# Second-layer weight sums paced at one per tick beside the memory heads, and no VectorE marks for sums among the value products

## The chip, the cores and the metric

The kernel runs on one core of a Trainium2 chip. The metric is the device time of one execution in microseconds. A core has TensorE (PE; weight loads are listed as PEld), VectorE (DVE), ScalarE (ACT), GpSimd (POOL) and SyncE (SP), each working through its own instructions in order, and 16 DMA engines that carry the transfers which SP and POOL issue. SP's transfers lie on a hardware queue (q1 in the profile), POOL's on a software queue (q0).

## The reference

Two post-norm layers over a sequence of 512 rows of width 2048. Each layer multiplies the stream by one wide input matrix and splits the result over three groups of heads; all outputs are gated, joined, projected and normalised:

```python
h = jnp.einsum('bsd,dn->bsn', x, w_in)
(fq, fk, fv, fg, f_logit, dq, dk, dv, dg, iq, ik, iw, mq, mg) = jnp.split(h, offsets, axis=-1)
# 6 forgetting heads: causal softmax with a cumulative log-forget bias
# 6 sparse heads: rotary q and k; an indexer of 16 heads chooses the keys of each query
# 4 memory heads: cross attention into mem (256 rows), whose k and v come from mem @ w_mem_kv
y = jnp.concatenate([y_fox * silu(fg), y_dsa * silu(dg), y_mem * silu(mg)], axis=-1)
y = jnp.einsum('bsn,nd->bsd', y, w_out)
return layer_norm(ALPHA * x + y, ln_gain, ln_bias)
```

## The kernel before

**Precision and chunks.** Every weight comes from DRAM as a chunk of 128 x 2048 fp32 (1 MB). `load_w` (L241) fetches it on SP's queue into a tile `raw` (three buffers). `split_w` makes of each half a rounded part `whi` (ACT, L213) and a remainder `wlo` (DVE, L214), four buffers each; `product` (L220 to L222) multiplies with three matmuls, hi x hi, hi x lo and lo x hi. Loads run two chunks ahead of the products, splits three halves.

**Stages of a layer.** Memory keys and values, small columns, the indexer's queries (stage "index"), the queries and gates of the four memory heads ("mem"), the values and other columns as large products ("values", kind `vs`), the remaining heads ("heads"), the output projection ("out"). The tuple `now` holds the layer and the stage.

**The value products.** These 512-column blocks are computed with seven products of sums of blocks where eight of plain blocks would be needed. That takes sums of weight blocks as right-hand sides. Some are formed in DRAM ahead of time: `weight_sums` copies a block into a DRAM tile `sum` (L376) and adds a second block by a DMA that accumulates (L358, 1 MB). Per layer the values need 32 such transfers: T3, eight copies and eight additions, then T1, likewise. T3 serves the product P7, T1 serves Q5, which comes after the first ten chunks of all four pairs. The two other right-hand sides are grown in place: when P7's chunk has been split, `grow_w` adds the next block into the same `raw` tile by an accumulating DMA (L249), which makes Q6's operand, and once more for Q4. A pair's first ten chunks are P1, P1, P7, P7, P2, Q6, Q6, P2, Q4, Q4; a value chunk holds 24 matmuls.

**What orders the DMAs of POOL.** POOL issues its DMAs in program order: weight sums, grows, the stores of value blocks (L874) and, in layer 1, the stores of the residual rows (L969). So that a sum is not issued long ahead of the place in the program where it stands, `pool_waits` puts a tiny copy on DVE (L348, the mark) and a tiny POOL operation that reads it (L349, seen) ahead of each sum. POOL then goes on only when DVE has come to that place.

**Pace.** `all_sums` is a generator that is stepped by `tick`. The main loop ticks twice per chunk; the sums skip the tick in a chunk's middle in the stages "out" and "values". After each sum `paced` yields the number of ticks until the next: two in "index" of layer 1 and one in "index" of layer 0, three in "out", one in "heads", two in "values", and in "mem" the expression that the change edits: `1 + now[0] * n % 2` is 1 in layer 0, and in layer 1 alternately 2 and 1.

**Layer 1 alone.** During "index" and "mem" of layer 1 `residual_rows` takes layer 0's normalised output through SBUF: SP loads 256 KB (L977), DVE multiplies and adds (L967, L968), POOL stores it (L969), 16 tiles, one every two ticks, with eight rows of gains and biases (L922).

Of the kernel before, what the change touches and what calls it, by code (L numbers as in the profile page):

```python
# [172 lines left out]
def kernel(  # L173
# [25 lines left out]
    def uid(name):  # L199
        count[0] += 1  # L200
        return f"{name}_{count[0]}"
# [7 lines left out]
    def small(name, w, bufs=3):  # L209
        return tiny.tile([P, w], F32, tag=name, name=uid(name), bufs=bufs)  # L210
# [134 lines left out]
    def pool_waits():  # L345

        mark, seen = small("mark", 1), small("seen", 1)
        nc.vector.tensor_copy(mark, mhalf)  # L348
        nc.gpsimd.tensor_tensor(seen, mark, mhalf, op=ALU.mult)  # L349
# [4 lines left out]
    def block(kind, l, pair, g, step):  # L354
        return wall[where[kind, l, 2 * pair + step[1], 2 * step[0] + g]]

    def add_weights(key, src):
        nc.gpsimd.dma_start(sums[key], src, accum_op=ALU.add, max_dma_last_dim=4 * DM)  # L358

    def weight_sums(kind, l, names, pairs):  # L360

        for name in names:
            for n, step in enumerate(SUM_STEPS[name]):
                for pair in pairs:
                    for g in range(2):
                        key = (kind, l, name, pair, g)
                        if isinstance(step, str):
                            src = sums[kind, l, step, pair, g]
                        else:
                            src = block(kind, l, pair, g, step)  # L370
                        pool_waits()
                        if n:
                            add_weights(key, src)
                        else:
                            sums[key] = dram.tile([P, DM], F32, name=uid("sum"))
                            nc.gpsimd.dma_start(sums[key], src)  # L376
                        yield

    def paced(gen, steps=2):

        n = 0
        for _ in gen:
            n += 1
            while now[1] == "kv":
                yield 1
            yield {"mem": 1 + now[0] * n % 2, "heads": 1, "out": 3, "index": 1 + now[0]}.get(now[1], steps)

    def all_sums():


        for l in range(DEPTH):
            yield from paced(weight_sums("val", l, ("T3", "T1"), range(PAIRS)))
            while now != (l, "heads"):
                yield 1
            yield from paced(weight_sums("out", l, ("T3", "T1", "T2", "T4"), range(2)))
# [7 lines left out]
    now = (0, "index")  # L403
# [646 lines left out]
    for i, (kind, l, j, col, _) in enumerate(chunks):  # L1050
# [28 lines left out]
        for h in range(2):  # L1079
            n = 2 * i + h  # L1080
# [135 lines left out]
        if kind == "mv" and l > 0:  # L1216
            now = (l, "kv")
        if kind == "small":
            now = (l, "index")
# [3 lines left out]
        if kind == "mq" and j == 0:  # L1223
            now = (l, "mem")
        if kind == "vs":
            now = (l, "values")
# [17 lines left out]
        if kind == "out" and step == col == 0:  # L1244
            now = (l, "out")
        if kind == "fq" and j == EARLY:
            now = (l, "heads")
# [111 lines left out]
```

## Time and profile before

| | |
|---|---|
| median of 3 runs | 1935.96 us (1935.47 to 1936.17) |
| the profiled execution's own time | 1936.96 us |
| its span, first to last instruction | 1934.6 us |
| mean granted clock of TensorE | 0.994 |
| busy: PE, PEld, DVE, ACT, POOL | 1907.3, 1624.6, 1389.3, 969.2, 356.0 us |
| marks (L348) and their reads on POOL (L349) | 128 each |
| weight sums: copies (L376) and additions (L358) | 64 each |

A row of the timeline gives the start and the length in us, engine, line, operation, what is written and read, and in brackets how long the engine stood idle ahead of it and whom it waited for. Grouped rows give a count (x), the busy time and the mean of one. In the table by stretches each engine's busy time stands with its number of instructions; then the granted clock of TensorE, the mean busy share of the 16 DMA engines, and GB/s. Line numbers are those of the kernel before; the change adds one line at L371, so in its own rows the lines behind have numbers one higher.

### The profile page before, as it was taken

What the parts mean: (1) busy time and instruction counts of PE and PEld (TensorE: products, weight loads), DVE (VectorE), ACT (ScalarE), POOL (GpSimd) and SP (SyncE); (2) the same over time, 40 slices, a digit from 0 to 9 for tenths busy, and PEclk for the clock granted to TensorE, in tenths of its full rate; (3) what the DMA queues carried; (4) which work ended last, traced back from release to release, by engine and by line L of the source; (5) the groups of instructions that cost most, each with busy time, mean ns of one, the idle gap of its engine ahead of it and who ended that gap; (6) DMA issues with size and microseconds to landing.
All of it is one profiled execution on the core that took longest, in us unless ns stands there. A gap on an engine that the chain in (4) does not pass through costs nothing.

```text
span 1934.6 us, 25323 instructions
## 1 busy us (share of the span) xinstructions
PE 1907.3 (99%) x9282; PEld 1624.6 (84%) x9282; DVE 1389.3 (72%) x2343; ACT 969.2 (50%) x1538; POOL 356.0 (18%) x615
## 2 busy tenths in 40 slices
PE   9999999999999999999999999899999999999997
PEld 8998888888888888888899988678888888888886
DVE  6666656779665667788867877367786656677898
ACT  6564454445444555645475644344454445555553
POOL 0231201111132111110142202111111331112101
PEclk9999999999999999999999999999999999999999
DMA  9699888787988778988778967898889887789856
GB/s 369 227 293 330 203 200 230 237 236 244 265 266 229 237 241 232 271 322 300 241 268 251 300 222 214 190 255 243 230 247 262 257 236 240 238 238 260 348 195 154
DMA packets 110712, 484.57 MB, mean 250 GB/s; under 512 B 11504, under 2 KB 44272, under 8 KB 69500
## 3 DMA queue, kind: packets, MB, share of 16 engines
q0 software_dynamic: 32864, 216.05, 44.7%
q1 hardware_dynamic: 77724, 266.90, 38.0%
q8 instruction: 73, 1.20, 0.2%
q14 instruction: 51, 0.42, 0.1%
HBM read 445.14 MB, written 174.09 MB: 320 GB/s over the span
## 4 chain that ended last, share of the span: by engine, by line
PE 90%; DVE 4%; DMA 2%; ACT 2%; issue 1%; POOL 0%; SPq 0%; DVEq 0%; ACTq 0%; POOLq 0%
PE c L220 12%; PE c L222 12%; PE c L221 12%; PE v L220 11%; PE v L222 11%; PE v L221 11%; PE z L221 4%; PE z L222 4%; PE z L220 4%; DMA raw<-in_wall_dram 2%; PE pt L681 1%; DVE wlo L214 1%; PE ix L599 1%; PE ix L598 1%; PE po L222 1%
## 5 line engine op out<-in xcount | busy, mean ns | idle before, releaser
L214 DVE TENSOR_TENSOR wlo<-raw,whi 128x1024 fp32r<-128x1024 f32 (+1 forms) x497 | 607.1, 1226 | 302.8 <-ACT whi L213 300.4
L213 ACT ACTIVATE whi<-raw 128x1024 fp32r<-128x1024 f32 (+1 forms) x497 | 521.2, 1054 | 397.6 <-PE v L222 215.8
L220 PE MATMUL c<-xh,whi 128*128 128x512 f32 (+1 forms) x1056 | 402.5, 381 | 0.0
L222 PE MATMUL c<-xh,wlo 128*128 128x512 f32 (+1 forms) x1056 | 398.6, 377 | 0.0
L221 PE MATMUL c<-xl,whi 128*128 128x512 f32 (+1 forms) x1056 | 397.7, 377 | 0.0
L222 PEld LDWEIGHTS c<-xh,wlo 128*128 128x128 f32 x1056 | 198.2, 188 | 32.3
L221 PEld LDWEIGHTS c<-xl,whi 128*128 128x128 f32 x1056 | 198.6, 188 | 30.5
L220 PEld LDWEIGHTS c<-xh,whi 128*128 128x128 f32 x1056 | 198.4, 188 | 29.9
L220 PE MATMUL v<-whi,vxh 128*128 128x512 f32 x512 | 201.2, 393 | 4.0 <-ACT whi L213 4.0
L221 PE MATMUL v<-wlo,vxh 128*128 128x512 f32 x512 | 200.5, 392 | 0.5 <-DVE mark L348 0.5
L222 PE MATMUL v<-whi,vxl 128*128 128x512 f32 x512 | 200.4, 391 | 0.0
L349 POOL TENSOR_TENSOR seen<-mark,mhalf 128x1 f32<-128x1 f32 x128 | 36.3, 284 | 811.1 <-DVE mark L348 777.3
L221 PE MATMUL z<-wlo,yh 128*128 128x512 f32 (+1 forms) x434 | 168.3, 388 | 2.5 <-DVE wlo L214 2.5
L220 PE MATMUL z<-whi,yh 128*128 128x512 f32 (+1 forms) x434 | 168.6, 388 | 0.0
L222 PE MATMUL z<-whi,yl 128*128 128x512 f32 (+1 forms) x434 | 167.9, 387 | 0.0
L220 PE MATMUL v<-whi,xh 128*128 128x512 f32 x384 | 150.6, 392 | 7.1 <-DVE vraw L851 7.1
L221 PE MATMUL v<-wlo,xh 128*128 128x512 f32 x384 | 150.5, 392 | 0.0
L222 PE MATMUL v<-whi,xl 128*128 128x512 f32 x384 | 150.4, 392 | 0.0
L220 PEld LDWEIGHTS v<-whi,vxh 128*128 128x128 f32 x512 | 96.8, 189 | 24.5 <-ACT whi L213 4.4
L221 PEld LDWEIGHTS v<-wlo,vxh 128*128 128x128 f32 x512 | 96.7, 189 | 20.9 <-DVE wlo L214 1.0
L222 PEld LDWEIGHTS v<-whi,vxl 128*128 128x128 f32 x512 | 96.7, 189 | 20.1
L221 PEld LDWEIGHTS z<-wlo,yh 128*128 128x128 f32 x434 | 81.6, 188 | 20.3 <-DVE wlo L214 4.2
(220 smaller groups left out, 3035.4 us busy)
## 6 DMA issues: line engine op xcount, KB each, us to landing
raw<-in_wall_dram SPq DMA_DIRECT2D x151, 1024.0 KB, 7.5
sum<-in_wall_dram POOLq DMA_DIRECT2D x64, 1024.0 KB, 10.8
raw<-sum SPq DMA_DIRECT2D x64, 1024.0 KB, 6.4
raw<-in_wall_dram POOLq DMA_DIRECT2D x32, 1024.0 KB, 8.0
v<-vraw POOLq DMA_DIRECT2D x96, 256.0 KB, 4.2
vraw<-v SPq DMA_DIRECT2D x64, 256.0 KB, 6.8
x<-z POOLq DMA_DIRECT2D x32, 256.0 KB, 7.6
memraw<-in_memt_dram SPq DMA_DIRECT2D x16, 256.0 KB, 7.2
```

Source lines behind the costliest of these rows:

```text
L213: nc.scalar.activation(hi, src, AF.Copy)
L214: nc.vector.tensor_tensor(lo, src, hi.bitcast(F32), op=ALU.subtract)
L220: nc.tensor.matmul(ps, ah, bh, start=start, stop=False, skip_group_check=more)
L221: nc.tensor.matmul(ps, ah, bl, start=False, stop=False, skip_group_check=more)
L222: nc.tensor.matmul(ps, al, bh, start=False, stop=stop, skip_group_check=more)
L349: nc.gpsimd.tensor_tensor(seen, mark, mhalf, op=ALU.mult)
L598: nc.tensor.matmul(o, st[:, qb * P:(qb + 1) * P], kh2[:, :w], start=True, stop=False)
L599: nc.tensor.matmul(o, st[:, qb * P:(qb + 1) * P], kl2[:, :w], start=False, stop=True)
L681: nc.tensor.transpose(tp[tb][:, toff + (qb - kt) * P:toff + (qb - kt + 1) * P], pr[b][:, off + kt * P:off + (kt + 1) * P], ident)
```

## The change

```diff
                             src = sums[kind, l, step, pair, g]
                         else:
                             src = block(kind, l, pair, g, step)
-                        pool_waits()
+                        if now[1] != "values":
+                            pool_waits()
                         if n:
                             add_weights(key, src)
                         else:
...
             while now[1] == "kv":
                 yield 1
-            yield {"mem": 1 + now[0] * n % 2, "heads": 1, "out": 3, "index": 1 + now[0]}.get(now[1], steps)
+            yield {"mem": 1, "heads": 1, "out": 3, "index": 1 + now[0]}.get(now[1], steps)
```

In "mem" of layer 1 a sum is issued at every tick. Sums whose place is among the value products get no mark. Layer 0's order is the same before and after, and so are the orders of PE, ACT and SP. The mark is copied 128 times in both programs.

POOL at the end of layer 1's memory heads and the beginning of its value products, before (`sum` is a weight sum, `raw` a weight tile that is grown, `x` a residual row's store, `v` a value block's store):

```order
L349 TENSOR_TENSOR seen_11467<-mark_11466,mhalf 128x1
L358 DMA sum_10669<-in_wall_dram 128x2048
L249 DMA raw_11431<-in_wall_dram 128x2048
L349 TENSOR_TENSOR seen_11585<-mark_11584,mhalf 128x1
L358 DMA sum_10809<-in_wall_dram 128x2048
L249 DMA raw_11479<-in_wall_dram 128x2048
L349 TENSOR_TENSOR seen_11671<-mark_11670,mhalf 128x1
L358 DMA sum_10871<-in_wall_dram 128x2048
L249 DMA raw_11431<-in_wall_dram 128x2048
L249 DMA raw_11479<-in_wall_dram 128x2048
L349 TENSOR_TENSOR seen_11750<-mark_11749,mhalf 128x1
L358 DMA sum_11041<-in_wall_dram 128x2048
```

and with the change:

```order
L358 DMA sum_10736<-in_wall_dram 128x2048
L970 DMA x_167<-z_11213 128x512
L349 TENSOR_TENSOR seen_11365<-mark_11364,mhalf 128x1
L358 DMA sum_10821<-in_wall_dram 128x2048
L970 DMA x_167<-z_11323 128x512
L249 DMA raw_11451<-in_wall_dram 128x2048
L249 DMA raw_11494<-in_wall_dram 128x2048
L249 DMA raw_11451<-in_wall_dram 128x2048
L249 DMA raw_11494<-in_wall_dram 128x2048
L875 DMA v_160<-vraw_11748 128x512
L875 DMA v_160<-vraw_11633 128x512
L875 DMA v_160<-vraw_11751 128x512
```

The four sums that stood ahead of, between and behind the first four grows are gone from there, with their reads of marks; the grows follow each other, and the last sum stands ahead of the last residual store.

POOL in the memory heads of layer 1, around the mask of the indexer's scores (L612 to L618), before:

```order
L969 DMA x_167<-z_10747 128x512
L349 TENSOR_TENSOR seen_11038<-mark_11037,mhalf 128x1
L376 DMA sum_11041<-in_wall_dram 16x16384
L969 DMA x_167<-z_10917 128x512
L612 MEMSET acc_10002 128x128
L613 AFFINE_SELECT acc_10002<-acc_10002 128x128
L618 AFFINE_SELECT acc_10003<-acc_10003 128x128
L618 AFFINE_SELECT acc_10002<-acc_10002 128x128
L618 AFFINE_SELECT acc_10004<-acc_10004 128x128
L349 TENSOR_TENSOR seen_11119<-mark_11118,mhalf 128x1
L358 DMA sum_10239<-in_wall_dram 128x2048
L969 DMA x_167<-z_11064 128x512
```

and with the change:

```order
L349 TENSOR_TENSOR seen_10818<-mark_10817,mhalf 128x1
L377 DMA sum_10821<-in_wall_dram 16x16384
L349 TENSOR_TENSOR seen_10880<-mark_10879,mhalf 128x1
L358 DMA sum_10239<-in_wall_dram 128x2048
L970 DMA x_167<-z_10759 128x512
L349 TENSOR_TENSOR seen_10987<-mark_10986,mhalf 128x1
L358 DMA sum_10360<-in_wall_dram 128x2048
L349 TENSOR_TENSOR seen_11054<-mark_11053,mhalf 128x1
L358 DMA sum_10474<-in_wall_dram 128x2048
L970 DMA x_167<-z_10928 128x512
L613 MEMSET acc_10002 128x128
L614 AFFINE_SELECT acc_10002<-acc_10002 128x128
```

The first additions stand here behind that mask before, and ahead of it with the change; between two residual stores stand up to two sums now, where there was one.

DVE at the first value products of layer 1, before (`wlo` is a weight half's remainder, `vxl` an operand's, `y` a memory head's output):

```order
L214 TENSOR_TENSOR wlo_11569<-raw_11546,whi_11568 128x1024
L348 COPY mark_11584<-mhalf 128x1
L795 SCALAR_TENSOR_TENSOR vxl_11566<-vx_11424,vxh_11565 128x512
L214 TENSOR_TENSOR wlo_11592<-raw_11546,whi_11591 128x1024
L214 TENSOR_TENSOR wlo_11608<-raw_11431,whi_11607 128x1024
L447 SCALAR_TENSOR_TENSOR y_11388<-po_11627,tanh_11373 128x256
L447 SCALAR_TENSOR_TENSOR y_11390<-po_11627,tanh_11373 128x256
L214 TENSOR_TENSOR wlo_11639<-raw_11431,whi_11638 128x1024
L214 TENSOR_TENSOR wlo_11655<-raw_11479,whi_11654 128x1024
L348 COPY mark_11670<-mhalf 128x1
L214 TENSOR_TENSOR wlo_11679<-raw_11479,whi_11678 128x1024
L214 TENSOR_TENSOR wlo_11695<-raw_11676,whi_11694 128x1024
```

and with the change, from the same place on:

```order
L214 TENSOR_TENSOR wlo_11584<-raw_11561,whi_11583 128x1024
L796 SCALAR_TENSOR_TENSOR vxl_11581<-vx_11444,vxh_11580 128x512
L214 TENSOR_TENSOR wlo_11602<-raw_11561,whi_11601 128x1024
L214 TENSOR_TENSOR wlo_11618<-raw_11451,whi_11617 128x1024
L448 SCALAR_TENSOR_TENSOR y_11408<-po_11637,tanh_11398 128x256
L448 SCALAR_TENSOR_TENSOR y_11410<-po_11637,tanh_11398 128x256
L214 TENSOR_TENSOR wlo_11649<-raw_11451,whi_11648 128x1024
L214 TENSOR_TENSOR wlo_11665<-raw_11494,whi_11664 128x1024
L214 TENSOR_TENSOR wlo_11684<-raw_11494,whi_11683 128x1024
L214 TENSOR_TENSOR wlo_11700<-raw_11681,whi_11699 128x1024
```

Two marks are gone. The second of them stood behind the remainder of a half of a grown tile (`raw_11479`, the second that is grown, its first half).

## Prediction

> **What bounds the kernel now.** I read the page first, then the list of waits of TensorE, then the two layers' value products side by side. From the page, the engines' busy time and the chain that ended last:
>
> ```profile
> PE 1907.3 (99%) x9282; PEld 1624.6 (84%) x9282; DVE 1389.3 (72%) x2343; ACT 969.2 (50%) x1538; POOL 356.0 (18%) x615
> PE 90%; DVE 4%; DMA 2%; ACT 2%; issue 1%; POOL 0%; SPq 0%; DVEq 0%; ACTq 0%; POOLq 0%
> ```
>
> TensorE sets the time nearly everywhere, so an edit pays only where TensorE stands still or runs slowly. The timeline of PE shows where that is: the first and the last row of the value products of layer 0 and of layer 1 (the last is the first matmul of the stage behind them), and two rows between.
>
> ```profile
> 249.40 0.40 PE L220 MATMUL v<-whi,xh 128*128 128x512 f32 x1
> 557.29 0.39 PE L220 MATMUL c<-xh,whi 128*128 128x512 f32 x1
> 1200.63 0.40 PE L220 MATMUL v<-whi,xh 128*128 128x512 f32 x1
> 1239.73 0.80 PE L220 MATMUL v<-whi,vxh 128*128 128x512 f32 x1 [4.01 <-ACT whi L213]
> 1261.37 0.77 PE L220 MATMUL v<-whi,xh 128*128 128x512 f32 x1 [7.09 <-DVE vraw L851]
> 1525.94 0.39 PE L220 MATMUL c<-xh,whi 128*128 128x512 f32 x1
> ```
>
> Both layers do the same products. Layer 0 takes 557.29 - 249.40 = 307.89 us, layer 1 takes 1525.94 - 1200.63 = 325.31 us: **17.4 us** more. Two waits stand in it, 4.01 and 7.09 us. The rest is the clock. In the table by stretches (length, busy time of PE, PEld, DVE, ACT, POOL, then granted clock, DMA share and GB/s):
>
> ```profile
> 1235.70:1239.80 4.10, 0.09 (x2) 0.07 (x1) 0.09 (x1) 1.18 (x2) 0.00 (x0) 0.92 0.12 24
> 1239.20:1246.00 6.80, 5.80 (x13) 4.23 (x14) 4.69 (x5) 3.32 (x4) 3.69 (x4) 0.50 0.40 72
> 1246.00:1254.20 8.20, 8.20 (x37) 6.50 (x35) 0.00 (x0) 0.00 (x0) 0.00 (x0) 1.00 0.97 238
> 1256.20:1266.50 10.30, 5.13 (x12) 4.10 (x13) 7.00 (x12) 4.00 (x4) 3.04 (x6) 0.50 0.74 147
> ```
>
> Behind each wait the granted clock is 0.50 for a while. Busy time there is worth half: 5.80 / 2 + 5.13 / 2 = 5.5 us lost. With the idle 4.0 + 7.1 + some 0.5 of small waits that is 17.1, and the comparison of the layers says 17.4. So the loss is explained: two late operands and their half-speed wake. The Trainium skill ("TensorE: Matmul & The Clock Gate", Part 1) states that an idle window of about 3.4 us halves the clock; the rows agree, and by that rule a leftover wait shorter than this would cost itself alone.
>
> **Why the operands are late.** POOL's timeline in layer 1 (L358 and L376 are weight sums, L349 the wait for a mark, L249 the accumulation into a weight tile that TensorE needs, below "grow"), then ACT and DVE, then two pieces of the chain (start, length):
>
> ```profile
> 1213.18 0.91 POOL L249 DMA_DIRECT2D raw<-in_wall_dram  x1 [3.75 <-DVE wlo L214]
> 1220.15 0.83 POOL L358 DMA_DIRECT2D sum<-in_wall_dram  x1
> 1220.71 1.21 POOL L249 DMA_DIRECT2D raw<-in_wall_dram  x1
> 1241.08 1.09 POOL L349 TENSOR_TENSOR seen<-mark,mhalf 128x1 f32<-128x1 f32 x1 [19.16 <-DVE mark L348]
> 1242.13 0.82 POOL L358 DMA_DIRECT2D sum<-in_wall_dram  x1
> 1242.69 2.09 POOL L249 DMA_DIRECT2D raw<-in_wall_dram  x2
> 1263.64 0.83 POOL L358 DMA_DIRECT2D sum<-in_wall_dram  x1
> ...
> 1238.62 3.90 ACT L213 ACTIVATE whi<-raw 128x1024 fp32r<-128x1024 f32 x4 [11.71 <-DMA raw<-in_wall_dram]
> 1258.31 2.00 ACT L213 ACTIVATE whi<-raw 128x1024 fp32r<-128x1024 f32 x2 [15.79 <-DMA raw<-in_wall_dram]
> ...
> 1239.71 1.23 DVE L214 TENSOR_TENSOR wlo<-raw,whi 128x1024 fp32r<-128x1024 f32 x1 [11.54 <-ACT whi L213]
> 1240.85 0.15 DVE L348 COPY mark<-mhalf 128x1 f32<-128x1 f32 x1
> ...
> 1220.71 17.81 DMA raw<-in_wall_dram
> 1242.69 15.52 DMA raw<-in_wall_dram
> ```
>
> Read it as a loop. The second grow is issued 0.56 us behind a sum and lands after 17.81 us, at 1238.5. ACT (11.71) and through it DVE (11.54) wait for it. The next mark stands on DVE behind that very split, so POOL waits 19.16 us for the mark, and the third and fourth grow stand on POOL behind the mark and another sum. They start at 1242.69 and land 15.52 us or more later: the second gap of TensorE.
>
> **What the change does.** Only layer 1's memory heads pace differently: a sum at every tick, not at every 1.5 on average. The same 128 marks stand in both programs' orders. The edit that drops marks among the values finds none to drop, because the four sums issued there (at 1208.6, 1220.2, 1242.1 and 1263.6, of which three are in the rows above) have moved ahead; I cost it at nothing, with no cover needed. PE, ACT and SP keep their orders. On POOL the first four grows now follow each other; on DVE the marks stand earlier. Marks cost 0.15 us on DVE (row above), and DVE is busy 45.5 of 60 us there (row below), so moving them is free. What is queued on POOL behind the earlier waits for marks are the residual rows' stores (L969); nobody waits for one but the slot of its tile, one of 71, so a store some microseconds later costs nothing.
>
> *Removed among the values.* Layer 0 is already the layout that layer 1 gets: every sum ahead, grows without marks between. Its rows on POOL, the first and last of its eight last sums and its four grows, and the grows' median landing there and in layer 1 (1206 to 1264 us):
>
> ```profile
> 195.45 0.84 POOL L358 DMA_DIRECT2D sum<-in_wall_dram  x1
> 240.99 0.80 POOL L358 DMA_DIRECT2D sum<-in_wall_dram  x1
> 261.89 0.90 POOL L249 DMA_DIRECT2D raw<-in_wall_dram  x1 [20.11 <-DVE wlo L214]
> 266.77 0.87 POOL L249 DMA_DIRECT2D raw<-in_wall_dram  x1 [3.97 <-DVE wlo L214]
> 275.84 0.86 POOL L249 DMA_DIRECT2D raw<-in_wall_dram  x1 [8.21 <-DVE wlo L214]
> 281.70 0.86 POOL L249 DMA_DIRECT2D raw<-in_wall_dram  x1 [5.00 <-DVE wlo L214]
> ...
> raw<-in_wall_dram POOLq DMA_DIRECT2D x4, 1024.0 KB, 8.4
> ...
> raw<-in_wall_dram POOLq DMA_DIRECT2D x4, 1024.0 KB, 16.7
> ```
>
> Layer 1's values start 1200.63 - 249.40 = 951.2 us later. Shifted so, layer 0's grows would be issued at 1213.1, 1218.0, 1227.1 and 1232.9; measured are 1213.2, 1220.7 and twice 1242.7. With 8.4 us to land, the second would be there at 1226.4. It landed at 1238.5 and TensorE then waited 4.0, so it may land as late as 1234.5: 8 us of margin. The third would land at 1235.5, far ahead of 1258.2. For the first grow, whose landing no pace of marks altered, the trace has a bound (landings in a stretch of 1 us around its issue):
>
> ```profile
> raw<-in_wall_dram POOLq DMA_DIRECT2D x1, 1024.0 KB, 10.6
> ```
>
> Those 10.6 us were with a sum issued 4.6 us ahead of it, and TensorE had no gap before 1235. So all 17.4 us should go.
>
> *Added to the memory heads.* Placed by their neighbours on DVE, the last eight sums would be issued at about 1146, 1156, 1164, 1170, 1174, 1181, 1188 and 1193. Layer 0's, shifted by 951.2, run from 1146.7 to 1192.2: the same pace. Their price: in layer 0 the software queue's share over 195 to 255 us, which holds these eight and nothing else, and both layers' last 60 us ahead of the values' loads (1146 to 1206 answers to layer 0's window):
>
> ```profile
> q0 software_dynamic: 1152, 8.39, 68.8%
> ...
> 195.00:255.00 60.00, 60.00 (x294) 50.70 (x293) 38.98 (x80) 27.61 (x60) 10.88 (x21) 1.00 0.87 210
> 1146.00:1206.00 60.00, 60.00 (x294) 50.69 (x293) 45.46 (x88) 27.46 (x60) 12.63 (x22) 1.00 0.78 222
> ```
>
> One sum costs 0.688 x 60 / 8 = 5.2 us of all DMA engines. Layer 1's window had 0.78 x 60 = 46.8 us of work with four such sums and two first copies; with eight and no copy it has 46.8 + 4 x 5.2 = 67.4 us less the two copies, which lie between 0 and 5.2 us each (estimate: 2.5, since a copy reads one operand fewer): 57 to 67 us, 62 taken. That is 2 us over the window, so the last sum should land at about 1208 to 1211, ahead of the first grow at 1213. Against layer 0, layer 1 also carries the residual rows' loads and stores here, which is the difference. Nothing on PE is lost while it runs: layer 0 at a DMA share of 0.87 has 60.00 of 60.00 us of PE busy. The bounds of this part: 0 us lost, or, at 67, a backlog of 7 us that reaches 1213 to 1216 and delays the first two grows by up to 3 us, within the 8 of the second.
>
> The Trainium skill ("DMA: Bandwidth & Descriptors", Queues, rings and completion order) speaks against the change: each DMA engine takes the queues in turn by packets, so denser sums slow SP's weight loads beside them. Layer 0's 60.00 busy us agree that these loads have the lead to bear it; by the rule too the sum stays.
>
> **Sum.** The profiled execution took 1936.96 us with a span of 1934.6. Less 17.4 it is 1919.6, and from the median of the runs, 1.0 lower, 1935.96 - 17.4 = **1918.6 us**, 0.9% faster. Nothing behind the values can take it back, since the chain is TensorE's there too (the page's 90%).
>
> **Rivals.**
>
> 1. *Half stays.* The residual rows' traffic pushes the eight sums beyond 1213, the second grow lands after 1234.5, and the first gap remains with its slow clock: 4.0 + 0.5 + 2.9 = 7.4 us. The loop through the mark is gone, so the second gap is not repeated: gain 10, about 1926. For it: by the sum above the engines have 62 us of work in 60, and up to 67. Against: 8 us of margin.
>
> 2. *No gain.* The grows are late because the engines are full in the values anyway, not because of sums or marks. Then 1936. Against: layer 0 has the same loads and stores there and no gap.
>
> 3. *Slower: the sums become dearer when packed.* One mechanism: accumulating sums in flight together, with SP's loads and the residual rows between, cost more than 5.2 us each, and the backlog runs into the first grows. Four sums in the values, 20.6 us of DMA, cost 17.4 us of TensorE. From (20.6 - 2) / 8 = 2.3 us dearer each (7.5) the backlog is as large and the gain is gone; at 9 us each it is 2 + 8 x 3.8 = 32 us, which at the same rate costs 27 us: 1918.6 + 27 = 1946. Against: layer 0's 5.2 us was measured at the same spacing, loads included.
>
> **How the numbers follow.** Full gain 0.78 with its own range of 1917 to 1921 (layer 0's pace is the best to be had; 1 us between runs); half 0.14; none 0.03; slower 0.05. The range reaches into the half case: 1917 to 1926. Faster by over 0.2% (3.9 us, what a measurement can tell from none): 0.92; within: 0.03; slower: 0.05.
>
> **What would show it.** Layer 1's value products take 308 us like layer 0's; PE has no wait over 1 us in them, no stretch there with a clock under 1.00; the four grows land within 8 to 11 us, the third issued at about 1227; no L349 stands between them. The memory heads show a DMA share near 1.0 with PE fully busy. Wrong would be a PE wait between 1110 and 1200, or a gap at 1235 again with a grow landing over 16 us after its issue.

## The result

The changed kernel takes **1919.19 us** (median of 4 runs, 1918.99 to 1920.01) against 1935.72 us of the kernel before (median of 4 runs, 1933.31 to 1936.17): a ratio of 0.9918, 95% interval 0.9901 to 0.9935. The forecast was 1918.6 us. The profiled execution took 1918.99 us with a span of 1916.8, 17.8 us less than the span before.

Where the time went can be read in four views of the changed kernel. From the page, TensorE's row and two groups of its waits over the whole span (the list of waits of PE):

```profile
PE 1900.9 (99%) x9282; PEld 1620.7 (85%) x9282; DVE 1389.3 (72%) x2343; ACT 969.6 (51%) x1538; POOL 355.8 (19%) x615
...
PE z L221 <- DVE wlo L214: 2.5, 4, 0.7
PE v L220 <- ACT whi L213: 0.2, 1, 0.2
```

The same matmuls were done with less busy time, 1900.9 in place of 1907.3 us: layer 1's value products, where nothing runs at half clock any more, account for 5.9 us of that (307.89 us busy in place of 313.74). The waits of 7.1 and 4.0 us are gone. The first row of layer 1's value products and of the stage behind them, and that stretch in the table by stretches (length, busy time of PE, PEld, DVE, ACT, POOL, clock, DMA share, GB/s):

```profile
1200.34 0.40 PE L220 MATMUL v<-whi,xh 128*128 128x512 f32 x1
1508.23 0.39 PE L220 MATMUL c<-xh,whi 128*128 128x512 f32 x1
...
1200.00:1508.00 308.00, 308.00 (x1370) 255.15 (x1369) 224.31 (x328) 146.98 (x172) 50.09 (x72) 1.00 0.87 242
```

1508.23 - 1200.34 = 307.89 us, to the hundredth what layer 0 took before, with a clock of 1.00 throughout. They start where they started before (1200.34 against 1200.63), so the memory heads lost nothing. What was saved is 325.31 - 307.89 = 17.4 us in this stage.

POOL's timeline there, with the last sum, the last residual store and the first four grows, and the DMAs issued from 1206 to 1264 and from 1146 to 1206 us (count, size, median us to landing), then the latter stretch:

```profile
1193.26 0.84 POOL L358 DMA_DIRECT2D sum<-in_wall_dram  x1
1203.05 0.59 POOL L970 DMA_DIRECT2D x<-z  x1 [8.96 <-DVE z L969]
1214.16 0.87 POOL L249 DMA_DIRECT2D raw<-in_wall_dram  x1 [10.53 <-DVE wlo L214]
1219.02 0.87 POOL L249 DMA_DIRECT2D raw<-in_wall_dram  x1 [3.99 <-DVE wlo L214]
1226.82 0.85 POOL L249 DMA_DIRECT2D raw<-in_wall_dram  x1 [6.92 <-DVE wlo L214]
1233.67 0.86 POOL L249 DMA_DIRECT2D raw<-in_wall_dram  x1 [6.00 <-DVE wlo L214]
...
raw<-in_wall_dram POOLq DMA_DIRECT2D x4, 1024.0 KB, 8.6
...
sum<-in_wall_dram POOLq DMA_DIRECT2D x8, 1024.0 KB, 14.1
raw<-sum SPq DMA_DIRECT2D x2, 1024.0 KB, 14.2
...
1146.00:1206.00 60.00, 60.00 (x293) 50.69 (x293) 45.38 (x89) 27.61 (x60) 15.73 (x26) 1.00 0.99 251
```

The grows land after 8.6 us (median) in place of 16.7, and the third is issued at 1226.8 in place of 1242.7. The price is in the memory heads: the DMA engines are busy at 0.99 in place of 0.78, a sum takes 14.1 us to land in place of 9.3, and SP's weight loads 14.2 in place of 8.4. TensorE is busy 60.00 of 60 us there all the same.

### The profile page after: what moved, and what is told of

Read it like the earlier page. It is cut to its first block, busy times and chain, and to the rows that moved or that the text cites. A ratio compares the mean times of both kernels' runs of the same rounds, so it can differ in the third digit from the quotient of the medians.

```text
span 1916.8 us, 25327 instructions
## 1 busy us (share of the span) xinstructions
PE 1900.9 (99%) x9282; PEld 1620.7 (85%) x9282; DVE 1389.3 (72%) x2343; ACT 969.6 (51%) x1538; POOL 355.8 (19%) x615
## 4 chain that ended last, share of the span: by engine, by line
PE 93%; DVE 4%; ACT 2%; issue 1%; DMA 0%; SPq 0%; POOL 0%; DVEq 0%; ACTq 0%; POOLq 0%
PE c L220 12%; PE c L222 12%; PE c L221 12%; PE v L222 11%; PE v L220 11%; PE v L221 11%; PE z L221 4%; PE z L222 4%; PE z L220 4%; PE pt L682 1%; PE ix L600 1%; PE ix L599 1%; PE po L222 1%; PE po L221 1%; PE po L220 1%
```

## The experiments

The prediction's theory was that the loss needs two things at once: sums ahead of the grows in POOL's queue, and POOL's wait for marks that stand on DVE behind the split of a grown tile. Rival A was that the marks do it alone, rival B that the traffic does. The runs are compared by their medians and by the length of layer 1's value products, from their first matmul to the first of the next stage in each profiled execution; 307.89 us is the length without loss.

| kernel | median us | ratio to before (95%) | value products, us | lost there, us |
|---|---|---|---|---|
| before | 1935.72 | 1 | 325.31 | 17.4 |
| changed | 1919.19 | 0.9918 (0.9901 to 0.9935) | 307.89 | 0 |
| e1: four sums, no marks | 1923.46 | 0.9935 (0.9919 to 0.9952) | 312.21 | 4.3 |
| e2: four marks, no sums | 1919.70 | 0.9916 (0.9901 to 0.9931) | 308.74 | 0.9 |
| e3: two sums more ahead | 1923.77 | 0.9938 (0.9923 to 0.9953) | 312.68 | 4.8 |
| e4: four sums more ahead | 1935.71 | 0.9998 (0.9988 to 1.0007) | 323.51 | 15.6 |
| e5: two more behind the last store | 1925.08 | 0.9947 (0.9932 to 0.9962) | 313.16 | 5.3 |
| e6: three more behind it | 1930.91 | 0.9971 (0.9961 to 0.9981) | 319.57 | 11.7 |
| e7: old pace, four sums spread | 1918.77 | 0.9913 (0.9898 to 0.9928) | 307.89 | 0 |

The kernel before had medians of 1935.99 (13 runs, beside e1 to e4) and 1936.33 us (12 runs, beside e5 to e7); each ratio is to the runs beside it. The lengths of the value products come from one profiled execution each. The 0.9 us of e2 is no more than the spread of the runs: its 1919.24 to 1920.59 us overlap the changed kernel's.

### Sums without marks, marks without sums

The first drops the marks alone: it puts the old pace back (against the changed kernel):

```diff
-            yield {"mem": 1, "heads": 1, "out": 3, "index": 1 + now[0]}.get(now[1], steps)
+            yield {"mem": 1 + now[0] * n % 2, "heads": 1, "out": 3, "index": 1 + now[0]}.get(now[1], steps)
```

> The change's second half alone: the old pace, so four weight sums still stand among layer 1's first value products, but without their marks on VectorE. Theory of the prediction (the loss needs both the sums' traffic ahead of the grows and the wait for the mark): the second grow is issued at about 1219, one sum ahead of it, lands at 1231 to 1236 where TensorE needs it by 1234.5; the third at about 1227 with another sum ahead, 1242 to 1246; 0 to 8 us of the 17.4 remain: 1919 to 1927. Rival A (the marks alone delay the grows): no loss, 1919. Rival B (the traffic alone, whatever the marks): the loss stays, 1934 to 1936.

The second keeps the change and puts marks back where they were (in `all_sums`, behind the values' sums):

```diff
+            if l == 1:
+                while now != (1, "values"):
+                    yield 1
+                for _ in range(4):
+                    pool_waits()
+                    yield 2
```

> The changed kernel, with four marks and POOL's waits for them put back at their old places among layer 1's first value products, but no sums there (132 marks in all). Theory of the prediction: the second grow waits about 1 us for its mark, lands at about 1229; the third waits for a mark behind the second's split, is issued at about 1233 and lands by 1242, just in time: 1919 to 1921. Rival A (marks alone): third and fourth grow are late by over 10 us as before, 1928 to 1936. Rival B (traffic alone): 1919.

Sums alone lose 4.3 us, marks alone 0.9 at most, both together 17.4: neither rival, and not the sum of the two either. (Without marks the sums also come earlier than in the kernel before, the second at 1213.7 in place of 1220.2.) The timeline of POOL in e1, then ACT's wait for the second grow and TensorE's for ACT:

```profile
1213.15 0.90 POOL L249 DMA_DIRECT2D raw<-in_wall_dram  x1 [8.31 <-DVE wlo L214]
1213.71 1.21 POOL L358 DMA_DIRECT2D sum<-in_wall_dram  x1
1218.01 0.90 POOL L249 DMA_DIRECT2D raw<-in_wall_dram  x1 [3.10 <-DVE wlo L214]
1218.56 1.21 POOL L358 DMA_DIRECT2D sum<-in_wall_dram  x1
1227.10 0.89 POOL L249 DMA_DIRECT2D raw<-in_wall_dram  x1 [7.33 <-DVE wlo L214]
...
1235.95 3.90 ACT L213 ACTIVATE whi<-raw 128x1024 fp32r<-128x1024 f32 x4 [10.40 <-DMA raw<-in_wall_dram]
...
1237.06 0.50 PE L220 MATMUL v<-whi,vxh 128*128 128x512 f32 x1 [1.30 <-ACT whi L213]
```

Without marks every grow is issued when its tile is split, the third at 1227.1 as in the changed kernel. Behind the sums the second still lands only at 1235.9, inside the 1231 to 1236 expected, and TensorE waits 1.3 us. In e2 the loop through the marks is there, without the traffic:

```profile
1221.19 0.88 POOL L249 DMA_DIRECT2D raw<-in_wall_dram  x1
1233.03 1.09 POOL L349 TENSOR_TENSOR seen<-mark,mhalf 128x1 f32<-128x1 f32 x1 [10.97 <-DVE mark L348]
1234.07 1.75 POOL L249 DMA_DIRECT2D raw<-in_wall_dram  x2
```

POOL waits 10.97 us for a mark behind the second grow's split, and the third grow is issued 7 us later than it could be; but the second lands early enough that this just suffices. So the marks turn one late grow into the next one's late issue: they pass a delay on, and without a delay they cost next to nothing.

### How much more traffic the grows bear

Two and four more sums, into DRAM tiles that nothing reads any more, at the last tick ahead of the values (`K` is 2 or 4):

```diff
+            if l == 1:
+                for g in range(K):
+                    pool_waits()
+                    add_weights(("val", 0, "T1", g // 2, g % 2), block("val", 1, g // 2, g % 2, (0, 0)))
+                yield 1
```

> The changed kernel with two weight sums more, issued at the last tick ahead of layer 1's values (about 1199 us), into a DRAM tile that nothing reads any more. Tests the margin of the first grows, with no mark among them. Theory of the prediction: at 5.2 us each the last sum lands at about 1223 in place of 1212.5; the first grow then lands at about 1228, the second at about 1233, which is inside the margin of 1234.5: 0 to 3 us lost, 1919 to 1922. Rival A (marks alone): 1919. Rival B: as the theory.

> The changed kernel with four weight sums more at the last tick ahead of layer 1's values (about 1199 us), into DRAM tiles that nothing reads any more. Theory of the prediction: the last sum lands at about 1233, the first grow at about 1238 and the second at about 1243, 8 us beyond its limit; one gap of 8 to 10 us and a stretch at half clock behind it, 11 to 15 us lost: 1930 to 1934. Rival A (marks alone): 1919. Rival B (traffic alone): 1930 to 1936.

With no mark among the grows, four more sums undo the whole gain: the loss is 15.6 us, a little over the 11 to 15 expected. That excludes rival A once more. It does not part the theory from rival B, whose forecast here was nearly the same: enough sums packed ahead of the grows do it without marks. ACT's wait for the first grow in e4 and TensorE's wait:

```profile
1242.54 1.06 ACT L213 ACTIVATE whi<-raw 128x1024 fp32r<-128x1024 f32 x1 [21.33 <-DMA raw<-in_wall_dram]
...
1244.13 0.80 PE L220 MATMUL v<-whi,vxh 128*128 128x512 f32 x1 [13.49 <-ACT vraw L850]
```

The gap stands at the first grow, which landed at 1242.4, and not at the second as expected. The row puts TensorE's wait down to a copy of ACT (`vraw`), which stands on ACT right behind the split of that tile.

e3 lost 4.8 us where 0 to 3 were expected, and in another place than expected: ahead of any grown tile. ACT and PE in e3:

```profile
1225.03 0.63 ACT L799 ACTIVATE vxh<-vx 128x512 fp32r<-128x512 f32 x1 [7.26 <-DMA x<-z]
...
1226.66 0.50 PE L220 MATMUL v<-whi,xh 128*128 128x512 f32 x1 [1.82 <-ACT whi L213]
```

ACT waits for a residual row's store (`x<-z`), issued at 1203.3 behind the added sums and landed at 1225.0: by the trace's releases the tile of that row had the slot that the value products' operand `vxh` gets next. The split that TensorE needs stands behind that operand on ACT. In e4 the same store took 33.6 us to land, and the same operand did not wait for it:

```profile
1217.53 0.62 ACT L799 ACTIVATE vxh<-vx 128x512 fp32r<-128x512 f32 x1
```

So this wait belongs to e3; it seems that the slots fall differently in the two kernels, which no view shows. To see whether this wait makes e3's loss, the added sums were issued behind that store (`K` is 2 or 3):

```diff
+            if l == 1:
+                while now != (1, "values"):
+                    yield 1
+                for g in range(K):
+                    add_weights(("val", 0, "T1", g // 2, g % 2), block("val", 1, g // 2, g % 2, (0, 0)))
+                yield 1
```

> Two weight sums more, as in the run with two more sums, but issued right behind the last residual row's store on POOL (about 1203.6 us, no marks) in place of ahead of it. In that run TensorE stood still from 1224.8 on, and ACT had waited 7.3 us for the landing of that store, whose tile's slot it needed: ahead of any grow. Slot theory: the store lands by 1215 as in the changed kernel, the gap at 1224.8 is gone, and what is left is the first grow landing at about 1230, where TensorE comes to it at 1230.6 and the split takes 1 to 2 us: 1 to 3 us lost, 1920 to 1922. Traffic theory (the loads and grows are late, whoever waits): the gap stays at about 1225, 1923 to 1925.

> The same with three sums more behind the store. The last sum lands at about 1229, the first grow at about 1235, 5 us behind the moment at which TensorE comes to it; with the half clock behind such a gap 7 to 10 us lost: 1926 to 1929. If the margin of the first grow were the 8 us that the prediction gave the second: 1 to 3 us, 1920 to 1922.

The gap at 1224.8 is gone, as the slot theory says, but its time isn't saved: e5 loses 5.3 us, more than the 1 to 3 which that theory allowed. The time of the traffic theory came about right (1925.08 us against 1923 to 1925), but not the place of its gap. The first grow now lands at 1231.5, 1.5 us later than expected, and TensorE, no longer held up before, comes to it in time to wait 2.82 us and then runs at half clock. In e3 the first grow had landed at 1229.9, so there the wait for the slot had covered this one, at least in part. With three sums the grow lands at 1237.3 and the wait is 8.71 us, 11.7 us lost where 7 to 10 were expected. ACT and PE in e5:

```profile
1231.64 1.06 ACT L213 ACTIVATE whi<-raw 128x1024 fp32r<-128x1024 f32 x1 [10.74 <-DMA raw<-in_wall_dram]
1232.60 1.07 ACT L851 ACTIVATE vraw<-v 128x512 f32<-128x512 f32 x2
...
1233.23 0.50 PE L220 MATMUL v<-whi,vxh 128*128 128x512 f32 x1 [2.82 <-ACT vraw L851]
```

and in e6:

```profile
1237.37 1.06 ACT L213 ACTIVATE whi<-raw 128x1024 fp32r<-128x1024 f32 x1 [16.53 <-DMA raw<-in_wall_dram]
...
1238.96 0.79 PE L220 MATMUL v<-whi,vxh 128*128 128x512 f32 x1 [8.71 <-ACT vraw L851]
```

TensorE starts 1.7 us behind the landing in both (1233.23 - 1231.5; 1238.96 - 1237.3). Without its wait it would have come to the tile 29.6 us behind the stage's first matmul in both. In the changed kernel, whose stage starts at 1200.34, that is 1230.0, so the first grow may land by 1228.3. It lands at 1222.2: a margin of about 6 us. The second grow has less. ACT's row for it in the changed kernel:

```profile
1229.92 2.01 ACT L213 ACTIVATE whi<-raw 128x1024 fp32r<-128x1024 f32 x2 [4.66 <-DMA raw<-in_wall_dram]
```

It lands at 1229.8. The prediction's limit of 1234.5, moved with the start of the stage, is 1234.2: a margin of 4.4 us. Two sums moved the two landings by 9.3 and 7.6 us in e5, so that both grows were some 2.8 us beyond their limits, and the wait for the first covered the second. By that (an estimate, no run adds a single sum) there is room for one sum more, not for two.

### The sums spread instead of packed

Is the packing into the memory heads what helps? The old pace and the marks stay here, and only the pace among the values changes (against the kernel before):

```diff
-            yield {"mem": 1 + now[0] * n % 2, "heads": 1, "out": 3, "index": 1 + now[0]}.get(now[1], steps)
+            yield {"mem": 1 + now[0] * n % 2, "heads": 1, "out": 3, "index": 1 + now[0], "values": 9}.get(now[1], steps)
```

> The kernel before (old pace in the memory heads, marks kept), but with nine ticks in place of two between the sums that are left for the values: the four stand about 49 us apart, the first at 1208.6 as before, the others behind the grows of a pair. Theory (a sum hurts only where it stands ahead of a grow that the DMA engines have no room for): one sum of 5.2 us among 49 us with a DMA share of 0.8 to 0.9 is absorbed, all of the loss is gone: 1918 to 1921. Rival (any sum among the values costs its share, 17.4 / 4 = 4.4 us): 1934 to 1936, or 1931 if the first one is free.

POOL at the first value products of e7, then the first and the last row of its value products:

```profile
1207.84 0.85 POOL L358 DMA_DIRECT2D sum<-in_wall_dram  x1
1212.45 0.91 POOL L249 DMA_DIRECT2D raw<-in_wall_dram  x1 [3.76 <-DVE wlo L214]
1217.31 0.87 POOL L249 DMA_DIRECT2D raw<-in_wall_dram  x1 [3.95 <-DVE wlo L214]
...
1257.94 0.88 POOL L358 DMA_DIRECT2D sum<-in_wall_dram  x1
...
1199.89 0.40 PE L220 MATMUL v<-whi,xh 128*128 128x512 f32 x1
1507.78 0.39 PE L220 MATMUL c<-xh,whi 128*128 128x512 f32 x1
```

307.89 us again: nothing is lost, with four sums and four marks among the values. One sum per 50 us finds room, even 4.6 us ahead of a grow; four within 55 us, between the grows of one pair, didn't. The time, 1918.77 us, cannot be told apart from the changed kernel's, since their intervals overlap. The rival, 4.4 us for each sum among the values, is excluded. No version beat the two, and there is nothing of this kind left to gain: TensorE is busy in all of layer 1's value products in either.

## Why the prediction was right, point by point

- **The place and the size.** Comparing the two layers gave 17.4 us as what the stage had lost; that came back in full. The span fell by 17.8 us; the median fell by 16.5, with runs of the kernel before spread over 1933.3 to 1936.2.
- **Layer 0 as the model.** Its grows, shifted by 951.2 us, were to be issued at 1213.1, 1218.0, 1227.1 and 1232.9; measured are 1214.2, 1219.0, 1226.8 and 1233.7. Their landing was to take 8.4 us and took 8.6 in the median, from 7.9 to 10.8. The sums were issued within 2 us of the places read from the order, the last at 1193.3.
- **The loop.** e1 and e2 show the step of the prediction that put the loss to sums and marks together: 4.3 and 0.9 us alone, 17.4 together. The half-gain rival's shape, one gap left when the loop is gone, is what e1 shows (4.3 us rather than 7.4); the changed kernel itself has no gap.
- **The dead half.** Dropping marks among the values found none to drop, as the order said. Had the pace not moved the sums, there would have been some to drop: e1 is that half alone, worth 13.1 of the 17.4 us.
- **The load on the memory heads.** 62 us of DMA work in 60, with 67 as the bound, was about right: the share was 0.99 and the last sum landed at 1212.5, just behind the forecast 1208 to 1211 and at the edge of the first grow's issue at 1214.2. A sum landed later when packed (14.1 us against 9.3 before), which is what the slower rival would begin with, and SP's loads slowed as the prediction had said. That is mostly waiting: the software queue took 71.3% of the 60 us, 42.8 us, for 8.82 MB. Less five stores of 0.26 MB, 7.5 MB or 7.2 sums are left, so even if the stores had cost nothing a sum took at most 6.0 us of the engines in place of 5.2. That rival needed 2.3 us more for each. The queue's row from 1146 to 1206 us (packets, MB, share):

```profile
q0 software_dynamic: 1389, 8.82, 71.3%
```

- **What was wrong in a step.** The margin was given as 8 us, for the second grow. It was 4.4: the grow was issued 1.0 us later than layer 0's rows said and took 10.8 us to land in place of 8.4. The first grow had about 6; for it the prediction had only the bound that 10.6 us to land had made no gap. The full gain came with about half the cover that was claimed for it, and e3 and e5 show that two sums more would have been too many. And it costed a late residual store at nothing since "nobody waits for one but the slot of its tile, one of 71". That held for TensorE in the changed kernel, where DVE waits for such a store without cost to it. It did not hold in e3, where a store's slot was asked for 14 us behind its issue and ACT stood still for 7.3 us. The row of DVE's wait is from the waits of the changed kernel between 1110 and 1275 us:

```profile
DVE vxl L777 <- DMA x<-z: 1.3, 1, 1.3
```

## What to carry to other kernels

Where two stages do the same work and one is slower, subtract them: the difference is the price, and the faster one shows what an edit can reach. A DMA that the bounding engine needs soon should not have more bulk transfers ahead of it in its queue than its margin covers (here one fitted in e7, and two did not in e5); in these runs bulk work was free where the queue had slack, packed or spread. A wait put in to keep such transfers in order should not stand behind the result of another of them, since it hands one delay on to the next.

## What the runs showed that I had not expected

**A short pause is enough for the half clock.** The prediction quoted the Trainium skill ("TensorE: Matmul & The Clock Gate", Part 1) for an idle window of about 3.4 us, and took from it that a wait shorter than that costs itself alone. In e1 the longest wait was 1.30 us, with one of 0.76 close behind. Two stretches of 3.41 us in e1, then two in e3:

```profile
1235.23:1238.64 3.41, 1.35 (x5) 0.58 (x4) 1.61 (x2) 2.69 (x3) 0.00 (x0) 1.00 1.02 199
1238.64:1242.05 3.41, 3.41 (x9) 2.64 (x8) 3.02 (x3) 1.20 (x2) 1.72 (x2) 0.50 1.03 209
...
1225.39:1228.80 3.41, 1.39 (x5) 0.94 (x6) 2.17 (x3) 2.16 (x3) 0.00 (x0) 1.00 1.00 207
1228.80:1232.21 3.41, 3.41 (x10) 2.63 (x9) 1.95 (x3) 2.24 (x4) 0.00 (x0) 0.50 1.01 219
```

A stretch in which TensorE was busy 1.35 or 1.39 of 3.41 us, about 40%, was followed by one of the same length at 0.50. TensorE need not stand still for the whole window, and the measurement decides: in these runs 2 us of pause within such a stretch cost 1.7 us more in clock, half of the 3.41 us that follow. From which busy share on the clock falls is not settled by these runs.

**A kernel's slots can connect what its queues don't.** e3 and the row of DVE above: a store of a finished stage held up an operand of the next one through the ring of 71 tiles; in e4, with the store later still, it did not. The waits of the kernel before show none of this kind at that place. Its last two stores landed after 9.4 and 6.6 us, against 17.2 and 11.7 in the changed kernel.
